# One layer of a conditioned trunk: second norm's root behind one modulation piece, transposes into bank pairs, ranking between queries, last rows loaded apart

## The chip, the cores and the metric

One Trainium2 chip, one of its cores. The metric is the device time of one execution of the program in microseconds (us), the median of several runs. The kernel before takes 3288.12 us, the median of three runs from 3284.90 to 3293.25. The profiled execution took 3291.78 us.

The engines are called as in the profile: PE multiplies matrices, PEld loads its weights, DVE works on vectors, ACT evaluates functions with a scale and a bias, POOL is the general engine that also issues the gathers, SP issues most DMAs.

## The reference

One layer, for 512 prompt rows (NA below) and 64 sample rows (8 groups of 8), with 2048 features each. It is cut here to what the change touches:

```python
mod = (silu(c) @ w_ada + b_ada).reshape(c.shape[0], 6, D_MODEL)
shift1, scale1, gate1, shift2, scale2, gate2 = [mod[:, k] for k in range(6)]
...
mix = concat([rmsnorm(out_lru), rmsnorm(out_sc)]) @ w_out
x = x + gate1 * mix
h2 = modulate(rmsnorm(x, norm2_g), shift2, scale2)
x = x + gate2 * peer(h2)
y = rmsnorm(x, final_g)
```

In `peer` each row has 8 heads. A head's query has two halves; each half is scored against 128 keys, the 16 best of each half make 256 candidates, and the 16 best of these pick 16 of 16384 experts. A pick multiplies the row with the expert's row of u, passes it through gelu and adds the expert's row of v, weighted.

## The kernel before, in words

All activations lie transposed: features on the 128 partitions, 16 chunks k of 128 features, the 576 rows along the free axis. Products that need full precision are made of three: every operand is split into a high and a low half (hhi, hlo; whi, wlo), and `mm3` (L131 to 139) multiplies high by high, low by high and high by low.

**Modulation pieces.** `w_ada` is read in 96 pieces of 1 MB (`ada_mm`, L181 to 192: load, four products into the bank `ada`, and after each fourth piece a copy `part` by ACT). `ada_out` (L194 to 208) transposes `part` into the bank `pm`, and DVE makes `pms` and the columns of `mods` of it. `ada_turn(n, keep)` (L351 to 361) does up to n pieces, leaves the last `keep` alone, and first finishes what is pending. The pieces are spread over the first stages as filling for PE.

**The w_out loop** (L611 to 630) runs over k: project chunk k into the PSUM tile `pp_o`, add the gated result to the row chunk `xk` to get `x1` (L622, L623 for the prompt rows, L624, L625 for the sample rows), write it to `x1d`, square it (L219) and add the squares into `sqa_n` (L220), and scale `x1` in place for the norm (L628, L629). An `ada_turn(1)` ends each pass.

**Norm 2.** `norm_stats` (L224 to 231) sums the squares over partitions on PE (`pc_n`, L228) and makes the reciprocal root `rc_n` on DVE and ACT (`rstd`, L140 to 149). `spread` (L233 to 241) multiplies it out over the partitions (`st_n`, L236, L238), and ACT copies it to `R_n` (L239, L240). Between the two stand `ada_turn(2, 0)` twice. Then the pieces that are left are done, and the last `pm` is transposed.

**The q loop** (L652 to 665), four passes q of four chunks each: `modulate` makes `m_h` (L283, DVE, every third chunk on POOL), `hhi` (L284, ACT) and `hlo` (L285, DVE); `mm3` adds these chunks into the first query's two banks `qa`; then PE transposes the new chunks back to rows, for the gathers' use, into `wide`, one tile of four banks, a bank for each 128 prompt rows i (L659). ACT copies the banks in pairs, after i = 1 and i = 3, to `h2s` (L663), and SP writes them to `h2d` (L665). `wide` has one buffer.

**The query stage** (L966 to 980) runs over seven heads: two projections each into a bank `qa` and a third of `wide`, ACT's copies, scores `sc`, and DVE's choice of the 16 best. From heads 0 to 3 DVE also counts how often a key scores high (`cnt`, L750). `rank_keys` (L930 to 959) is a generator in four parts: constants, the sum of the counts (`rk<-cnt`, L943), its transposition and the comparison (L948 on), and the permutation `perm` with `blk`, the order in which blocks of experts are read. The first part is run ahead of head 1, the other three after head 3, at high priority. Up to here PE's order in the w_out and q loops is as written; the other engines' order, and all of the query stage, is set by a scheduler.

**U and V stages** follow a schedule that is written out by hand: for each block of experts of the order `blk`, `pu` (L1367) and `pv` (L1387), with `xhi` and `xlo` (L900, L901) as halves of the loaded rows. Picks that miss the blocks are gathered row by row by POOL (L1197) and summed by DVE (u L1225, accB L1252), and the sums are scattered into `accd` in DRAM (L1267). `v_sum` (L1405 to 1421) adds a column `pv` of 128 features x 512 rows into `acc` (L1409), for eleven groups of heads (4, nine of 8, 4).

**The end.** In the last group (M - 4 to M - 1 of the M steps; `last` is M - 9) each column also takes in the gathered rows: `tok`, four tiles of 128 rows, loaded from `accd` at step last + 4 (L1725), transposed by PE onto `pv` (L1391). `v_sum` then scales by gate2 and adds (L1411), squares (L1415), writes the column to `x2d` (L1416), and sums the squares (L1421). `token_norm` (L1423 to 1438) makes the root of the last norm and spreads it into the bank `prfa`, copied to `sqs`, which is R (L1436). The last loop (L1758 to 1766) scales the 16 columns by `final_g` and R, every third one by ACT (L1762) and POOL (L1763), the others by DVE (L1765), and SP writes each to `y` (L1766).

Of the kernel before, what the change touches and what calls it, by code (L numbers as in the profile page):

```python
# [5 lines left out]
F32 = mybir.dt.float32  # L6
# [74 lines left out]
def build(ctx, tc, A, O, dbg=None):  # L81
# [532 lines left out]
    for k in range(KD):  # L614
# [9 lines left out]
        V.tensor_tensor(s3(x1[:, k, NP:]), s3(p[:, 1, NX:HT]), ctx_b(g1, k), op=ALU.mult)  # L624
        V.tensor_add(x1[:, k, NP:], x1[:, k, NP:], xk[:, NP:])  # L625
# [4 lines left out]
        ada_turn(1)  # L630
# [3 lines left out]
    ada_turn(2, 0)  # L634
    ada_turn(2, 0)
# [10 lines left out]
    wide = psum["p"].tile([128, 4, 512], F32, name="wide", tag="hT", bufs=1)  # L646

# [4 lines left out]
    for q in range(4):  # L652
# [3 lines left out]
        for i in range(NA // 128):  # L656
            for k in range(4):
                for p in range(2):
                    PE.matmul(wide[:, i, k * 128:(k + 1) * 128], hv[p][:, 4 * q + k, i * 128:(i + 1) * 128], idr,  # L659
                              start=p == 0, stop=p == 1)  # L660
            if i % 2:
                with tc.high_priority():
                    S.activation(t[:, i - 1:i + 1, :], wide[:, i - 1:i + 1, :], AF.Copy)  # L663
        for i in range(NA // 128):
            nc.sync.dma_start(h2d[i * 128:(i + 1) * 128, q * 512:(q + 1) * 512], t[:, i, :])  # L665
    pe1.close()
    dump("x1", x1)
# [250 lines left out]
    def query_banks(h, p):  # L918
        return [pbank("u", f"qa{h}{p}", 2)[:, :HT], wide[:, (2 * h + p) % 3, :HT]]
# [42 lines left out]
    for h in range(HD - 1):  # L962
        for p in range(2):
# [3 lines left out]
            if h or p:  # L967
                his, los = stream_w(A["wq"][2 * h + p], f"q{h}{p}")
                mm3(pq, his, los, movs)
            query_out(h, p, pq)  # L970
# [3 lines left out]
        if h == HEADS_COUNTED - 1:  # L974
            with tc.high_priority():
                run(ranking)
# [61 lines left out]
    def sample_rows():  # L1038

        hT = first_h["h"] = psum["p"].tile([128, D], F32, name="hT0", tag="hT", bufs=1)  # L1040
# [159 lines left out]
    def gather_u(i):  # L1200
# [8 lines left out]
        def use_h():  # L1209
            st["h"] = psum["p"].tile([128, D], F32, name=f"hT{i}", tag="hT", bufs=1)  # L1210
# [23 lines left out]
    def gather_v(i):  # L1234
# [7 lines left out]
        def add(j):  # L1242
            r, a = held.pop(j)
            row_log[a] = True
            if j == 0:
                S.activation(dots[i], dots[i], AF.Gelu_apprx_tanh)
                V.tensor_mul(dots[i], dots[i], gwt[i])
                st["a"] = psum["p"].tile([128, D], F32, name=f"accB{i}", tag="hT", bufs=1)
# [155 lines left out]
    def v_sum(gi, k, pv):  # L1404
# [5 lines left out]
        else:  # L1410
# [5 lines left out]
            nc.sync.dma_start(x2d[:, k, :], ak)  # L1416
            if k == 0:
# [5 lines left out]
    def token_norm(sq, n, nm, pool, banks):  # L1423
# [14 lines left out]
        return R  # L1438

    def finish_b():  # L1440
# [9 lines left out]
        ph = psum["p"].tile([128, D], F32, name="ph", tag="hT", bufs=1)  # L1450
# [257 lines left out]
    fplan = {(last + 1, 2), (last + 2, 3), (last + 3, 1), (last + 3, 3), (last + 4, 1), (last + 4, 3)}  # L1708
    NT = len(uses)
    cost = [FULL_ROWS if j < NU + bound[0] else 1.0 for j in range(NV0, NT)]  # L1710
    sums = [sum(cost[:j + 1]) for j in range(len(cost))]
    for m in range(M):
# [8 lines left out]
        if m == last + 4:  # L1721
            fin["tok"] = []
            for t in range(QT):
                r = new_row(f"tok{t}")[0]
                nc.sync.dma_start(r, accd[t * 128:(t + 1) * 128, :])  # L1725
# [175 lines left out]
```

## Time and profile before

| what | value |
|---|---|
| median of three runs | 3288.12 us (3284.90, 3288.12, 3293.25) |
| profiled execution, its own time | 3291.78 us |
| its span | 3290.0 us |
| mean granted PE clock | 0.972 |
| busy POOL / ACT | 1711.0 us (52%) / 1056.4 us (32%) |
| HBM read / written | 879.89 MB / 66.81 MB, 288 GB/s over the span |
| chain that ended last, shares | PE 42%, DMA 14%, issue 5%, DVE 4%, POOL 3%, ACT 1% |

A row of the waits reads: engine, tile and line that waited, the engine, tile and line that it waited for, the time in all, how many times, the longest. A row of the timeline reads: start, duration, engine, line, operation, tile written and tiles read, shapes, count, and in brackets the idle time before it and what ended that. A row of the windows gives for each engine its busy time and the count of instructions, then the granted PE clock, the busy share of the DMA engines and what they moved. In the tile names of the trace `x` is x1 as well as the chunks added to it, and `sqs` are the three tiles of the last norm.

### The profile page before, as it was taken

The numbers are of one execution on the slowest core, as the hardware profiler recorded it, in microseconds if no ns is written. First come the engines' busy times: TensorE is split into PE (matmuls) and PEld (weight loads), VectorE is DVE, ScalarE is ACT, GpSimd is POOL, SyncE is SP. The second block draws the span as 40 slices with busy tenths as digits, with TensorE's granted clock in tenths as the row PEclk, the third lists the DMA queues.
The fourth block names the chain that finished last, engine by engine and source line by source line (L and its number), as shares of the span: only waits on it lengthen the run. The fifth ranks groups of instructions, "written<-read, shape, count | busy, mean of one in ns | idle before, by whom it ended". The sixth has DMA issues, their size and how long they took to land.

```text
span 3290.0 us, 46694 instructions
## 1 busy us (share of the span) xinstructions
PE 3098.8 (94%) x17239; PEld 2625.0 (80%) x17239; DVE 2200.9 (67%) x3265; ACT 1056.4 (32%) x1645; POOL 1711.0 (52%) x1000
## 2 busy tenths in 40 slices
PE   6899999999979999999999998998999998989897
PEld 2688898999969998887788887886887777767676
DVE  3465521153345898896998989866777786877845
ACT  3244311132232232232565555642322222122122
POOL 2233233344333235667556665656677686676742
PEclk8999999999979999999999999999999999999998
DMA  9744565624432227989779898989999988998963
GB/s 378 259 144 134 165 220 199 223 93 132 130 129 80 71 85 251 309 311 380 311 307 388 357 374 318 395 289 388 394 367 395 389 326 308 346 351 322 373 201 142
DMA packets 297067, 882.84 MB, mean 268 GB/s; under 512 B 37590, under 2 KB 79446, under 8 KB 245366
## 3 DMA queue, kind: packets, MB, share of 16 engines
q1 hardware_dynamic: 161760, 382.48, 33.5%
q0 software_dynamic: 66336, 413.41, 31.8%
q10 hardware_dynamic: 68736, 83.90, 7.2%
q8 instruction: 136, 2.23, 0.3%
q14 instruction: 99, 0.81, 0.1%
HBM read 879.89 MB, written 66.81 MB: 288 GB/s over the span
## 4 chain that ended last, share of the span: by engine, by line
PE 42%; DMA 14%; issue 5%; DVE 4%; POOL 3%; ACT 1%; ACTq 0%; SPq 0%; POOLq 0%; DVEq 0%
PE pu L1367 17%; PE pv L1387 15%; DMA gsb<-gd 5%; DMA raw<-v 3%; PE qa L139 3%; DMA v<-v,rows 3%; PE wide L139 3%; PE gbank L1565 2%; POOL xlo L901 2%; DMA actr<-actd 2%; DMA u<-u,rows 1%; DVE u L1225 1%; POOL u L1197 1%; DVE accB L1252 1%; PE sc L736 0%
## 5 line engine op out<-in xcount | busy, mean ns | idle before, releaser
L901 POOL TENSOR_TENSOR xlo<-raw,xhi 128x1024 fp32r<-128x1024 f32 x320 | 777.1, 2441 | 455.8 <-ACT xhi L900 451.1
L900 ACT ACTIVATE xhi<-raw 128x1024 fp32r<-128x1024 f32 x320 | 338.5, 1060 | 873.4 <-PE pv L1387 418.3
L1252 DVE SCALAR_TENSOR_TENSOR accB<-v,dots,accB 128x2048 f32<-128x2048 f32 x211 | 496.4, 2353 | 160.5 <-DMA v<-v,rows 155.7
L1225 DVE SCALAR_TENSOR_TENSOR u<-u,hT 128x2048 f32<-128x2048 f32 x223 | 505.0, 2283 | 139.1 <-DMA u<-u,rows 137.1
L1387 PE MATMUL pv<-ahi,xhi 128*128 128x512 f32 x1280 | 515.3, 403 | 49.9 <-DVE acc L1409 38.5
L1387 PE MATMUL pv<-ahi,xlo 128*128 128x512 f32 x1280 | 510.7, 399 | 6.0 <-POOL xlo L901 6.0
L1367 PE MATMUL pu<-hhi,xhi 128*128 128x512 f32 x1280 | 515.8, 403 | 0.0
L1367 PE MATMUL pu<-hhi,xlo 128*128 128x512 f32 x1280 | 503.1, 393 | 5.9 <-POOL xlo L901 5.9
L1387 PE MATMUL pv<-alo,xhi 128*128 128x512 f32 x1280 | 507.7, 397 | 0.0
L1367 PE MATMUL pu<-hlo,xhi 128*128 128x512 f32 x1280 | 504.7, 394 | 0.0
L1387 PEld LDWEIGHTS pv<-ahi,xhi 128*128 128x128 f32 x1280 | 244.3, 191 | 115.5 <-DVE acc L1409 28.8
L1197 POOL DMA_INDIRECT u<-u,rows x223 | 226.0, 1014 | 201.9 <-DVE u L1225 154.3
L1197 POOL DMA_INDIRECT v<-v,rows x223 | 261.9, 1175 | 81.3 <-issue 37.5
L1387 PEld LDWEIGHTS pv<-ahi,xlo 128*128 128x128 f32 x1280 | 244.0, 191 | 66.1 <-POOL xlo L901 8.9
L1367 PEld LDWEIGHTS pu<-hhi,xlo 128*128 128x128 f32 x1280 | 241.7, 189 | 60.9 <-POOL xlo L901 6.8
L1387 PEld LDWEIGHTS pv<-alo,xhi 128*128 128x128 f32 x1280 | 244.8, 191 | 54.5
L1367 PEld LDWEIGHTS pu<-hhi,xhi 128*128 128x128 f32 x1280 | 242.5, 189 | 50.6 <-issue 0.9
L1367 PEld LDWEIGHTS pu<-hlo,xhi 128*128 128x128 f32 x1280 | 242.4, 189 | 47.4
L1559 ACT ACTIVATE op<-op,it 128x128 f32<-128x128 f32 x512 | 155.9, 389 | 72.4 <-DVE op L1551 70.0
L1565 PEld LDWEIGHTS gbank<-wr,op 128*128 128x128 f32 x1024 | 134.6, 193 | 39.5 <-ACT stg L1572 29.9
L1565 PE MATMUL gbank<-wr,op 128*128 128x80 f32 x1024 | 133.4, 274 | 23.5 <-ACT stg L1572 23.2
L128 POOL TENSOR_TENSOR wlo_q<-raw_q,whi_q 128x1024 fp32r<-128x1024 f32 x28 | 67.4, 2406 | 152.2 <-ACT whi_q L126 148.6
(481 smaller groups left out, 5512.0 us busy)
## 6 DMA issues: line engine op xcount, KB each, us to landing
wa<-w_ada SPq DMA_DIRECT2D x96, 1024.0 KB
raw<-ut SPq DMA_DIRECT2D x160, 512.0 KB
raw<-v SPq DMA_DIRECT2D x320, 256.0 KB
actd<-act ACTq DMA_DIRECT2D x80, 256.0 KB
gd<-stg ACTq DMA_DIRECT2D x64, 320.0 KB
gsb<-gd ACTq DMA_DIRECT2D x80, 256.0 KB
actr<-actd ACTq DMA_DIRECT2D x40, 512.0 KB
raw_o<-w_out SPq DMA_DIRECT2D x32, 512.0 KB
```

Source lines behind the costliest of these rows:

```text
L128: lo_engine(share).tensor_sub(lo, raw, r32(hi))
L139: PE.matmul(o, st, mv[pick](k), start=first, stop=last)
L900: S.activation(hi, raw, AF.Copy)
L901: G.tensor_sub(lo, raw, r32(hi))
L1197: G.indirect_dma_start(out=out, out_offset=None, in_=src, in_offset=bass.IndirectOffsetOnAxis(ap=idx, axis=0), bounds_check=NE * 128 - 1, ...
L1225: V.scalar_tensor_tensor(r, r, 1.0, st["h"], op0=ALU.mult, op1=ALU.mult, accum_out=dots[i][:, j:j + 1])
L1252: V.scalar_tensor_tensor(st["a"], r, dots[i][:, j:j + 1], st["a"], op0=ALU.mult, op1=ALU.add)
L1367: PE.matmul(pu, st[:, kk, :], movA[mv](k), start=k == 0 and a == 0, stop=k == KD - 1 and a == 2)
L1387: PE.matmul(pv, st, mv, start=first and j == 0 and a == 0, stop=last and not end and j == SG - 1 and a == 2)
L1559: S.activation(ops[:, j0 + j, :], ops[:, j0 + j, :], AF.Copy, scale=it[2][:, b * 4 + j:b * 4 + j + 1])
L1565: PE.matmul(pg[:, j * L:(j + 1) * L], ops[:, j0 + j, :], wr[:, j0 + j, :], start=True, stop=True)
```

## The change

It has five parts.

1. *Norm 2.* The sample rows' gated product is left in PSUM and added from there. `ada_turn(1, 6)` leaves six pieces instead of seven, so one more is done in the w_out loop; between root and spread stands one call of `ada_turn` for one piece, where two calls for up to two pieces each stood.
2. *Banks.* `wide` becomes a pool of its own with two-bank tiles in two buffers, one for each pair of i. It is closed after the loop, and the query stage gets a pool with four banks `qb` of its own. The tile `hT` and its successors move to a third pool.
3. *Ranking.* After query 0 of head 4, query 1 of head 4 and query 0 of head 5 one part of the generator is run, instead of the three parts after head 3.
4. *Gathered rows.* The four loads of `tok` stand at columns 0 and 2 of step last + 3 and of step last + 4.
5. *Last scaling.* ACT scales every third column (k % 3 == 1) right after its write to `x2d`, in place; `token_norm` also returns the bank that holds R, and DVE reads R there; POOL multiplies the scaled columns; odd columns are written to `y` by ACT's queue.

```diff
-        V.tensor_tensor(s3(x1[:, k, NP:]), s3(p[:, 1, NX:HT]), ctx_b(g1, k), op=ALU.mult)
-        V.tensor_add(x1[:, k, NP:], x1[:, k, NP:], xk[:, NP:])
+        V.tensor_tensor(s3(p[:, 1, NX:HT]), s3(p[:, 1, NX:HT]), ctx_b(g1, k), op=ALU.mult)
+        V.tensor_add(x1[:, k, NP:], p[:, 1, NX:HT], xk[:, NP:])
...
-        ada_turn(1)
+        ada_turn(1, 6)
     w_q = stream_w(A["wq"][0], "q00")
     ada_turn(2, 0)
     spread = norm_stats(st, D, "n2")
-    ada_turn(2, 0)
-    ada_turn(2, 0)
+    ada_turn(1, 0)
     R = spread()
...
-    wide = psum["p"].tile([128, 4, 512], F32, name="wide", tag="hT", bufs=1)
+    psw = ExitStack()
+    wp = psw.enter_context(tc.tile_pool(name="psw", bufs=1, space=PSUM))
...
         for i in range(NA // 128):
+            if i % 2 == 0:
+                wide = wp.tile([128, 2, 512], F32, name=f"wide{q}{i}", tag="wide", bufs=2)
             for k in range(4):
                 for p in range(2):
-                    PE.matmul(wide[:, i, k * 128:(k + 1) * 128], hv[p][:, 4 * q + k, i * 128:(i + 1) * 128], idr,
+                    PE.matmul(wide[:, i % 2, k * 128:(k + 1) * 128], hv[p][:, 4 * q + k, i * 128:(i + 1) * 128], idr,
                               start=p == 0, stop=p == 1)
             if i % 2:
                 with tc.high_priority():
-                    S.activation(t[:, i - 1:i + 1, :], wide[:, i - 1:i + 1, :], AF.Copy)
+                    S.activation(t[:, i - 1:i + 1, :], wide, AF.Copy)
...
     pe1.close()
+    psw.close()
+    psq = ExitStack()
+    qp = psq.enter_context(tc.tile_pool(name="psq", bufs=1, space=PSUM))
...
-        return [pbank("u", f"qa{h}{p}", 2)[:, :HT], wide[:, (2 * h + p) % 3, :HT]]
+        return [pbank("u", f"qa{h}{p}", 2)[:, :HT], qp.tile([128, 512], F32, name=f"qb{h}{p}", tag="qb", bufs=4)[:, :HT]]
...
                 mm3(pq, his, los, movs)
+            if 0 <= 2 * h + p - 2 * HEADS_COUNTED < 3:
+                with tc.high_priority():
+                    next(ranking)
             query_out(h, p, pq)
...
-        if h == HEADS_COUNTED - 1:
-            with tc.high_priority():
-                run(ranking)
...
             nc.sync.dma_start(x2d[:, k, :], ak)
+            if k % 3 == 1:
+                S.activation(ak, ak, AF.Copy, scale=cols[:, C_FG + k:C_FG + k + 1])
...
-        return R
+        return (R, pr[:, :n]) if nm == "a" else R
...
+    tplan = {(last + 3, 0), (last + 3, 2), (last + 4, 0), (last + 4, 2)}
...
-        if m == last + 4:
-            fin["tok"] = []
-            for t in range(QT):
-                r = new_row(f"tok{t}")[0]
-                nc.sync.dma_start(r, accd[t * 128:(t + 1) * 128, :])
-                fin["tok"].append(r)
...
+            if (m, kq) in tplan:
+                t = len(fin["tok"])
+                r = new_row(f"tok{t}")[0]
+                nc.sync.dma_start(r, accd[t * 128:(t + 1) * 128, :])
+                fin["tok"].append(r)
...
-        if k % 3 == 2:
-            S.activation(ak, ak, AF.Copy, scale=fg)
+        if k % 3 == 1:
             G.tensor_mul(ak, ak, R)
         else:
-            V.scalar_tensor_tensor(ak, ak, fg, R, op0=ALU.mult, op1=ALU.mult)
-        nc.sync.dma_start(O["y"][:, k, :NA], ak)
+            V.scalar_tensor_tensor(ak, ak, fg, Rp, op0=ALU.mult, op1=ALU.mult)
+        (nc.scalar if k % 2 else nc.sync).dma_start(O["y"][:, k, :NA], ak)
```

The order of PE between the w_out loop and the first query, before (`ada` is the bank that collects four pieces `wa` of a quarter vector, `part` its copy, `pm` its transposition; `pc_n`, `rc_n`, `st_n` belong to norm 2, `qa` to the first query):

```order
L228 MATMUL pc_n_8157<-ones,sqa_n_6369 128x1 x5
L189 MATMUL ada_2_5773<-wa_2_3_8171,cpad 32x512 x4
L199 MATMUL pm_2_8179<-ident,part_2_8177 128x128 x4
L189 MATMUL ada_3_8187<-wa_3_0_8188,cpad 32x512 x4
L189 MATMUL ada_3_8187<-wa_3_1_8194,cpad 32x512 x4
L236 MATMUL st_n_0_8201<-ident,rc_n_8163 128x128 x4
L238 MATMUL st_n_1_8202<-ident,rc_n_8163 128x64
L189 MATMUL ada_3_8187<-wa_3_2_8210,cpad 32x512 x4
L189 MATMUL ada_3_8187<-wa_3_3_8216,cpad 32x512 x4
L199 MATMUL pm_3_8224<-ident,part_3_8222 128x128 x4
L139 MATMUL qa_8241<-hhi,whi_q_0_8135 128x288
```

And now, on the same engine at the same place:

```order
L189 MATMUL ada_2_5773<-wa_2_3_8157,cpad 32x512 x4
L228 MATMUL pc_n_8165<-ones,sqa_n_6369 128x1 x5
L199 MATMUL pm_2_8179<-ident,part_2_8163 128x128 x4
L189 MATMUL ada_3_8187<-wa_3_0_8188,cpad 32x512 x4
L236 MATMUL st_n_0_8195<-ident,rc_n_8171 128x128 x4
L238 MATMUL st_n_1_8196<-ident,rc_n_8171 128x64
L189 MATMUL ada_3_8187<-wa_3_1_8204,cpad 32x512 x4
L189 MATMUL ada_3_8187<-wa_3_2_8210,cpad 32x512 x4
L189 MATMUL ada_3_8187<-wa_3_3_8216,cpad 32x512 x4
L199 MATMUL pm_3_8224<-ident,part_3_8222 128x128 x4
L139 MATMUL qa_8243<-hhi,whi_q_0_8141 128x288
```

The two products that make `st_n` stand behind one piece and one transposition, where they stood behind three pieces and one transposition; the piece `wa_2_3` is now ahead of `pc_n`, since every piece has moved up by one and one is done in the w_out loop.

ACT at the same place, before (`x` is the in-place scaling of the last chunk of x1, `R_n` the copy of the spread root, `ms_h_0` the sample rows of chunks 0 to 3):

```order
L192 ACTIVATE part_2_8177<-ada_2_5773 128x512
L628 ACTIVATE x_6307<-x_6307,mod_3369 128x512
L239 ACTIVATE R_n_8200<-st_n_0_8201 128x512
L240 ACTIVATE R_n_8200<-st_n_1_8202 128x64
L284 ACTIVATE hhi<-m_h_1_8248,mod_4442 128x512
L284 ACTIVATE hhi<-m_h_0_8244,mod_4442 128x512
L245 ACTIVATE hhi<-ms_h_0_8243 128x4x64
L284 ACTIVATE hhi<-m_h_2_8252,mod_4442 128x512
L284 ACTIVATE hhi<-m_h_3_8256,mod_4442 128x512
L192 ACTIVATE part_3_8222<-ada_3_8187 128x512
L284 ACTIVATE hhi<-m_h_4_8328,mod_4442 128x512
L284 ACTIVATE hhi<-m_h_5_8332,mod_4442 128x512
```

And now:

```order
L144 ACTIVATE rc_n_8171<-rc_n_8171 128x5
L239 ACTIVATE R_n_8194<-st_n_0_8195 128x512
L240 ACTIVATE R_n_8194<-st_n_1_8196 128x64
L628 ACTIVATE x_6307<-x_6307,mod_3369 128x512
L284 ACTIVATE hhi<-m_h_0_8246,mod_4442 128x512
L284 ACTIVATE hhi<-m_h_1_8250,mod_4442 128x512
L245 ACTIVATE hhi<-ms_h_0_8245 128x4x64
L284 ACTIVATE hhi<-m_h_2_8254,mod_4442 128x512
L284 ACTIVATE hhi<-m_h_3_8258,mod_4442 128x512
L284 ACTIVATE hhi<-m_h_4_8332,mod_4442 128x512
L284 ACTIVATE hhi<-m_h_5_8336,mod_4442 128x512
L192 ACTIVATE part_3_8222<-ada_3_8187 128x512
```

The last `part` copy, `part_3`, has moved behind the `hhi` of chunks 4 and 5; the scaling of `x` has moved behind the two copies of the root.

PE in the projection during which the sum of the counts is made, before (`rk` is the ranking's bank, `cnt` the counts, `qa` and `wide` the banks of the projection):

```order
L139 MATMUL qa_10080<-hlo,whi_q_0_10083 128x288
L139 MATMUL qa_10080<-hhi,wlo_q_0_10085 128x288
L943 MATMUL rk_9929<-cnt,ones 128x128
L139 MATMUL qa_10080<-hhi,whi_q_0_10083 128x288
L139 MATMUL wide<-hhi,whi_q_0_10083 128x288
L139 MATMUL wide<-hlo,whi_q_0_10083 128x288
```

And now, `qb` being the second bank:

```order
L139 MATMUL qb_10092<-hhi,whi_q_0_10095 128x288
L139 MATMUL qa_10091<-hlo,whi_q_0_10095 128x288
L947 MATMUL rk_10084<-cnt,ones 128x128
L139 MATMUL qb_10092<-hlo,whi_q_0_10095 128x288
L139 MATMUL qa_10091<-hhi,wlo_q_0_10097 128x288
L139 MATMUL qb_10092<-hhi,wlo_q_0_10097 128x288
```

The product of the counts is row 3943 of PE's order in both, the transposition `rk<-ident,rk_row` row 3952 in both; the last product, `rk<-rk_low,rowi`, has moved from row 3967 to row 4049. The banks of the projection alternate now where one was filled ahead of the other.

More of the change, by code (lines that the diff above doesn't have):

```diff
@@ L1038, in sample_rows @@
     def sample_rows():
-        hT = first_h["h"] = psum["p"].tile([128, D], F32, name="hT0", tag="hT", bufs=1)
+        psq.close()
+        psum["h"] = ctx.enter_context(tc.tile_pool(name="ps3", bufs=1, space=PSUM))
+        hT = first_h["h"] = psum["h"].tile([128, D], F32, name="hT0", tag="hT", bufs=1)
         for k in range(KD):
@@ L1209, in use_h @@
         def use_h():
-            st["h"] = psum["p"].tile([128, D], F32, name=f"hT{i}", tag="hT", bufs=1)
+            st["h"] = psum["h"].tile([128, D], F32, name=f"hT{i}", tag="hT", bufs=1)
             r, a = held.pop("h")
@@ L1247, in add @@
                 V.tensor_mul(dots[i], dots[i], gwt[i])
-                st["a"] = psum["p"].tile([128, D], F32, name=f"accB{i}", tag="hT", bufs=1)
+                st["a"] = psum["h"].tile([128, D], F32, name=f"accB{i}", tag="hT", bufs=1)
                 V.tensor_scalar(st["a"], r, dots[i][:, 0:1], None, op0=ALU.mult)
@@ L1449, in finish_b @@
         yield
-        ph = psum["p"].tile([128, D], F32, name="ph", tag="hT", bufs=1)
+        ph = psum["h"].tile([128, D], F32, name="ph", tag="hT", bufs=1)
         for k in range(KD):
@@ L1708, in build @@
     fplan = {(last + 1, 2), (last + 2, 3), (last + 3, 1), (last + 3, 3), (last + 4, 1), (last + 4, 3)}
+    fin["tok"] = []
+    tplan = {(last + 3, 0), (last + 3, 2), (last + 4, 0), (last + 4, 2)}
     NT = len(uses)
@@ L1755, in norm_banks @@
         return pbank("u", f"pcf{nm}", 2), pbank("g", f"prf{nm}", 2)
-    R = drive(token_norm(fin["sq"], NA, "a", vp, norm_banks("a")))
+    R, Rp = drive(token_norm(fin["sq"], NA, "a", vp, norm_banks("a")))
     for k in range(KD):
```

## The prediction

> **What bounds the kernel now.** I read the page first, then the windows of the whole program, then the waits of the stages that the change touches, then their timelines. On the page, the span and the busy shares:
>
> ```profile
> span 3290.0 us, 46694 instructions
> PE 3098.8 (94%) x17239; PEld 2625.0 (80%) x17239; DVE 2200.9 (67%) x3265; ACT 1056.4 (32%) x1645; POOL 1711.0 (52%) x1000
> ```
>
> The profiled execution took 3291.78 us, 1.8 more than its span and 3.7 more than the median of 3288.12; the sum below is made against 3291.78. PE is busy for 94% of it, so a gain must come from the 191 us in which PE stands, or from stretches in which it runs at a lower clock. The same, by stages (start:end, length, busy time of PE, PEld, DVE, ACT, POOL, granted clock, DMA share, GB/s):
>
> ```profile
> 943.00:1000.00 57.00, 47.30 (x262) 46.37 (x263) 18.83 (x28) 20.03 (x28) 22.93 (x16) 0.72 0.28 95
> 1000.00:1110.00 110.00, 109.98 (x822) 106.92 (x821) 72.31 (x465) 27.85 (x50) 35.80 (x15) 1.00 0.22 73
> 1110.00:1217.00 107.00, 100.96 (x729) 98.46 (x728) 104.44 (x448) 23.06 (x43) 34.03 (x14) 0.97 0.23 75
> 2290.00:3180.00 890.00, 844.22 (x3596) 676.78 (x3595) 684.64 (x395) 199.56 (x187) 609.36 (x361) 0.99 0.92 345
> ```
>
> The first is the q loop behind norm 2: 10 us idle and a mean clock of 0.72, the worst of the four. The second is the query stage, full to the brim. Who is waited for in the q loop, and how its windows of 3.4 us follow each other:
>
> ```profile
> PE wide L659 <- ACT h2s L663: 8.6, 5, 4.0
> 950.40:953.80 3.40, 0.00 (x0) 0.00 (x0) 3.37 (x5) 2.64 (x4) 2.69 (x3) 1.00 0.00 0
> 953.80:957.20 3.40, 3.33 (x16) 3.33 (x16) 3.16 (x3) 1.35 (x3) 3.24 (x4) 0.52 0.40 154
> 957.20:960.60 3.40, 3.40 (x16) 3.40 (x16) 1.34 (x2) 0.50 (x2) 2.76 (x3) 0.50 0.00 0
> 960.60:964.10 3.50, 2.93 (x24) 2.70 (x23) 2.63 (x5) 2.94 (x5) 0.09 (x1) 0.98 0.14 54
> 964.10:967.50 3.40, 1.64 (x15) 1.50 (x15) 1.40 (x2) 2.42 (x3) 3.40 (x3) 1.00 0.29 111
> 967.50:970.90 3.40, 3.40 (x17) 3.40 (x17) 0.00 (x0) 1.02 (x1) 3.40 (x3) 0.51 0.39 146
> 970.90:974.30 3.40, 3.40 (x16) 3.40 (x16) 0.00 (x0) 0.00 (x0) 2.49 (x2) 0.50 0.00 0
> 974.30:977.70 3.40, 2.34 (x20) 2.20 (x19) 0.00 (x0) 1.02 (x1) 0.00 (x0) 0.98 0.86 249
> 977.70:981.10 3.40, 3.35 (x16) 3.35 (x17) 0.00 (x0) 0.00 (x1) 0.00 (x0) 0.52 0.56 214
> 981.10:984.50 3.40, 3.40 (x16) 3.40 (x16) 0.00 (x0) 1.02 (x1) 0.00 (x0) 0.50 0.36 141
> ```
>
> Three windows hold over a microsecond of idle PE time (3.40, 1.76 and 1.06 us). Behind each stand two at clock 0.5, each doing in 3.4 us what takes 1.7 at full clock. A wait there costs itself and about 3.4 us more: six slow windows, 10.2 us.
>
> **The change part by part.** *The norm's root (ctx part through PSUM, one ada piece earlier).* The timeline round it:
>
> ```profile
> 920.75 2.31 DVE L625 TENSOR_TENSOR x<-x,xk 128x64 f32<-128x64 f32 x1
> 928.75 3.64 PE L189 MATMUL ada<-wa,cpad 128*32 128x512 f32 x16
> 932.33 1.68 PE L236 MATMUL st_n<-ident,rc_n 128*128 128x128 f32 x8
> 934.05 0.60 ACT L239 ACTIVATE R_n<-st_n 128x512 f32<-128x512 f32 x1 [5.78 <-PE st_n L236]
> 940.57 0.58 ACT L192 ACTIVATE part<-ada 128x512 f32<-128x512 f32 x1
> 943.66 1.33 ACT L284 ACTIVATE hhi<-m_h,mod 128x512 fp32r<-128x512 f32 x2 [2.52 <-POOL m_h L283]
> 941.20 1.12 PE L199 MATMUL pm<-ident,part 128*128 128x128 f32 x4 [3.53 <-ACT part L192]
> ```
>
> L625 takes 2.31 us for 64 columns with both operands in SBUF; with one from PSUM at most that can go, and the sum of squares behind it, whose operands stay in SBUF, may take the delay over: 0 to 2 us, I take 1. Then st_n stands behind one ada piece instead of three. The two that move away are worth one row: 3.64 us for two pieces, 1.82 each at the clock that they had. So R comes some 4.6 us earlier, near 929.4. None of it need reach PE: the last pm waits for the last ada part, and in the new order ACT does that part behind two more hhi, which in before begin at 943.66, 9.6 us behind R. With R at 929.4 these two end near 940.3, the part ends near 940.9, and pm begins near 941, as now. The piece that moves into the PE-bound k loop costs 0.9 us (half of 1.82, at full clock); one piece less stands behind the loop, where PE waits 3.53 us anyway. I take 0 for the part, between 1 lost (the piece, with nothing back) and 5 won (all of R's lead). If the hhi come later than that, PE's projections start later with them, which is the lost end.
>
> *Banks in pairs.* PE's third block of transposes no longer waits for the copy of the first two blocks, only for the copy of its own pair, a loop pass earlier. That removes the 8.6 us and the 10.2 behind them, 18.8. The copies themselves are still late once: ACT's order has them behind two hhi of 0.67, and the next query's banks open only when the last copy is out, as now:
>
> ```profile
> 992.17 0.61 PE L139 MATMUL wide<-hhi,whi_q 128*128 128x288 f32 x1 [1.11 <-ACT h2s L663]
> ```
>
> That wait stays, and I let one more of its size with its slow stretch (1.1 + 3.4) stay inside the loop: 14.3 us. Bounds: 18.8 if none is left, 5.3 if three are. The Trainium skill's page "TensorE: Matmul & The Clock Gate" (HAM oscillation, and its table of advice) says that only gaps of about 3 us and more bring the clock down. The trace disagrees: idle times of 1.76 and 1.06 us have the same two slow windows behind them as that of 3.40. If the rule held, short waits would not be what slows those windows, and this part would give 7.5; that is the first rival.
>
> *Query banks of their own* (four instead of three quarters of the wide tile) change nothing in a stage where PE is busy 109.98 of 110 us.
>
> *Ranking behind three queries.*
>
> ```profile
> 1115.21 0.77 PE L943 MATMUL rk<-cnt,ones 128*128 128x128 f32 x2 [4.85 <-DVE cnt L750]
> ```
>
> PE stands 4.85 us for DVE's count. In the new order the product of the count stands in the same row of PE's 13,000, the transposition too; only the third product moves 82 rows back, and no wait is shown there. DVE, 104.4 of 107 us busy, reaches its count no earlier against PE. I take 0; 8 if the wait and a slow stretch (4.85 + 3.4) went after all, and 1 lost if DVE's copies come late for the block numbers.
>
> *Gathered rows apart.*
>
> ```profile
> 3184.00:3188.00 4.00, 4.00 (x19) 3.03 (x18) 1.46 (x2) 0.22 (x1) 3.18 (x2) 1.00 0.56 197
> 3188.55 2.36 SPq L1725 DMA_DIRECT2D tok<-accd  x4
> PE pv L1391 <- DMA tok<-accd: 5.4, 3, 2.0
> 3197.06 0.38 PE L1391 MATMUL pv<-ident,tok 128*128 128x128 f32 x2
> 3204.91 5.12 PE pv L1387 x12
> 3211.04 2.79 PE pv L1387 x12
> ```
>
> Four loads of 1 MB begin at 3188.55; the first is used at 3197.06, the others are waited for. Two now start a step earlier, where the DMA queues are half idle (0.56), and two where all four were, with half the bytes ahead: the last two should land about when the first two did, at 3197 to 3199. The waits cost 5.4 us and the slow clock behind them 2.3 (5.12 for the same twelve products that take 2.79 a column later): 7.7. It is half of that if the last tile is still late, and a little more, 8.5, if the pairs between the waits also run at full clock. SP issues nothing later than before: xf goes from behind four of these loads to behind two and two.
>
> *The last scaling.*
>
> ```profile
> 3271.00 12.46 DVE L1765 SCALAR_TENSOR_TENSOR acc<-acc,cols,sqs 128x512 f32<-128x512 f32 x11 [2.86 <-ACT sqs L1436]
> 3227.03 0.74 DVE L1411 SCALAR_TENSOR_TENSOR acc<-pv,mod,acc 128x512 f32<-128x512 f32 x1
> 3270.00:3274.00 4.00, 0.33 (x2) 0.04 (x1) 3.00 (x3) 3.63 (x6) 2.35 (x2) 0.50 0.20 74
> 3282.00:3286.00 4.00, 0.00 (x0) 0.00 (x0) 1.46 (x3) 0.00 (x0) 0.00 (x0) 0.50 1.03 381
> 3286.00:3290.00 4.00, 0.00 (x0) 0.00 (x0) 0.00 (x0) 0.00 (x0) 0.00 (x0) 0.50 0.31 118
> 912.78 0.72 ACT L628 ACTIVATE x<-x,mod 128x512 f32<-128x512 f32 x1 [1.76 <-DMA x1d<-x]
> ```
>
> Eleven columns take 12.46 us, 1.13 each, from SBUF alone beside POOL. With R in PSUM a column has the operands of L1411, 0.74: 8.1 us, and they begin 0.6 earlier, since DVE no longer waits for ACT's copy of R (0.60, as the copy of R_n above, of the same shape). That would be 5.0. But the output is 4.2 MB, 11.0 us at the 381 GB/s of the only full window. Before, its traffic begins near 3273.2 (0.20 of that window, at its end) and ends near 3287.3 (0.31 of the last). It would now begin at 3272.6 and end at 3283.6: 3.7 us won. Bounds 3 and 5. Half of the writes move to ACT's queue, which has nothing else to do there. The scaling that ACT does early waits for the column's own write; it stood 1.76 us for such a write in the k loop and then took 0.72, together less than the 2.79 us that PE needs for a column's first twelve products. It is hidden; if the write took twice as long it would cost about 1.5 us in each of five columns.
>
> *Between them.* 14 us won at 990 must pass through 2200 us of query, U and V stages. All their loads are released by PE, DVE or POOL work of the same stage, so I let them shift whole.
>
> The sum: 0 + 14.3 + 0 + 7.7 + 3.7 = 25.7, so 3266.1 for the profiled execution and 3262.4 against the median; I say 3262.
>
> **The rivals.** *The clock stays low in the q loop.* Not the short waits but the kind of work (transposes with little in them) would hold the clock down; then two of the three slow pairs of windows, 6.8 us, stay. For it: the slow windows are filled with transposes (x16). Against: the slow rows behind 1.06 us of idle, and the projections of the window before it, which run at 0.98. 25.7 less 6.8 is 18.9: 3269. Chance 0.15.
>
> *The lead is lost on the way.* In U and V the DMA share is 0.92, and who sets the pace there may be bytes rather than PE. Then only the end counts, 7.7 + 3.7 = 11.4: 3277. Against it PE's 844 busy of 890. Chance 0.13.
>
> *The ranking works.* If DVE is ahead by as much as the norm's lead, the 4.85 and the slow stretch go as well, 8.2: 33.9 in all, 3254. Chance 0.07.
>
> *Slower: the V stage falls out of step.* Rows of the stage:
>
> ```profile
> DVE accB L1252 <- DMA v<-v,rows: 133.4, 52, 9.9
> PE pv L1387 <- DVE acc L1409: 38.5, 20, 5.5
> ```
>
> DVE does PE's sums and the gathered rows' sums in one queue. When a gathered row is late, up to 9.9 us, PE's sum stands behind it and PE's banks fill; that already costs 38.5 us. A shift of 14 us moves gathers against weight loads; were each of the nine groups of eight to get one more wait of the longest kind, 9 x 5.5 = 50 us would come on, and the total would be 3288 - 26 + 50 = 3312. It decides from 26 us of new waits on, five such. Against it: gathers and sums are placed by PE's steps and not by time. Chance 0.05.
>
> **How the numbers follow.** The forecast itself has 0.60. A measurement of this kernel tells 0.3% from no change, 9.9 us: faster is below 3278.2, slower above 3298. The forecast's own bounds (5.3 to 18.8, 3.9 to 8.5, 3 to 5, and -1 to 5 for the norm, not all at one end) run from 3252 to 3275. The lost lead at 3277, give or take 4, must be taken in, and the ranking at 3254: 3250 to 3280 leaves out the slower case and the edges, under 0.2. Faster: 0.57 + 0.14 + 0.08 + 0.07 = 0.86; same: 0.03 + 0.01 + 0.05 = 0.09; slower: 0.05.
>
> **What would show it.** In the new profile: PE's waits for h2s at 0 to 2 us instead of 8.6, and one slow pair of windows or none between 950 and 990; R_n near 929 to 930 but the first projection still near 942; the wait for cnt unchanged at 4.8; waits for the gathered rows under 1 us; the eleven last columns in about 8 us and the output ending about 11 us after its first byte. The prediction is wrong if PE's waits in the V stage move by more than 10 us either way, if the q loop keeps a clock near 0.7 without waits, or if ACT waits for the x2d writes beyond a column's pitch.

## The result, and the profile after

The changed kernel takes 3276.97 us, the median of twelve runs (3261.30 to 3283.48), beside 3294.31 for the kernel before, of twelve as well (3284.90 to 3303.69). The ratio is 0.994, 95% interval 0.9925 to 0.9954: 15 to 25 us won, 20 most likely (the two medians are 17.3 apart). The forecast was 25.7 and a time of 3262, in a range of 3250 to 3280. Of the 15 us between 3262 and 3277, 6 are the base: the three runs of before that the sum was set against had a median of 3288.12, and twelve have 3294.31.

The profiled execution took 3275.15 us. Its page:

```profile
span 3273.3 us, 46692 instructions
PE 3088.6 (94%) x17239; PEld 2616.8 (80%) x17239; DVE 2173.3 (66%) x3265; ACT 1056.9 (32%) x1645; POOL 1718.4 (52%) x1000
```

The span is 16.7 us shorter, PE's busy time 10.2: part of the gain is idle time, part is work that now runs at full clock.

**Norm 2.** The timeline between the w_out loop and the first query, of the changed kernel:

```profile
920.99 0.22 DVE L625 TENSOR_TENSOR x<-pp_o,xk 128x64 f32<-128x64 f32 x1
921.96 1.74 DVE L220 TENSOR_TENSOR sqa_n<-sqa_n,sq_n 128x576 f32<-128x576 f32 x1 [0.75 <-ACT sq_n L219]
927.79 1.93 PE L236 MATMUL st_n<-ident,rc_n 128*128 128x128 f32 x8
929.75 0.60 ACT L239 ACTIVATE R_n<-st_n 128x512 f32<-128x512 f32 x1 [4.28 <-PE st_n L236]
939.37 1.33 ACT L284 ACTIVATE hhi<-m_h,mod 128x512 fp32r<-128x512 f32 x2 [2.98 <-POOL m_h L283]
940.61 0.57 ACT L192 ACTIVATE part<-ada 128x512 f32<-128x512 f32 x1
941.23 1.12 PE L199 MATMUL pm<-ident,part 128*128 128x128 f32 x4 [6.98 <-ACT part L192]
```

L625 fell from 2.31 us to 0.22, and the sum of squares behind it took over a part of that (1.74 where it took 0.76). It seems to be POOL that holds them: before, its subtraction for `wlo_q` ran from 920.62 to 922.97, and L625, with both operands in SBUF, ended at 923.06; now it runs from 920.74 to 923.10, L625 with one operand in PSUM passes beside it in 0.22 us, and the sum of squares, still in SBUF alone, ends at 923.70. R comes at 929.75 instead of 934.05. PE sees nothing of it at this place: the last `pm` begins at 941.23, where it began at 941.20, and its wait has doubled, 6.98 us for 3.53.

**The q loop.** PE's waits in it, and its windows:

```profile
PE wide L660 <- ACT h2s L664: 1.8, 1, 1.8
PE qb L139 <- ACT h2s L664: 1.1, 1, 1.1
PE qa L139 <- ACT qt L927: 3.0, 1, 3.0
953.80:957.20 3.40, 2.16 (x20) 2.02 (x18) 3.03 (x4) 1.93 (x4) 1.28 (x1) 1.00 0.40 154
957.20:960.60 3.40, 2.81 (x22) 2.81 (x23) 3.03 (x5) 2.89 (x5) 1.68 (x1) 0.93 0.40 154
960.60:964.00 3.40, 3.40 (x18) 3.40 (x17) 0.00 (x0) 1.75 (x2) 3.40 (x3) 0.56 0.42 159
964.00:967.40 3.40, 3.40 (x33) 3.40 (x32) 0.00 (x0) 1.03 (x1) 3.40 (x3) 1.00 0.00 0
...
981.00:984.40 3.40, 1.51 (x10) 1.51 (x11) 0.65 (x5) 0.71 (x2) 0.00 (x0) 0.95 0.23 78
984.40:987.80 3.40, 3.40 (x17) 3.40 (x16) 0.00 (x0) 0.31 (x1) 0.00 (x0) 0.55 0.00 0
```

One wait for a copy is left of five, and one slow window stands behind it instead of six. (The two further executions of the kernel before have four slow windows there: the pair behind the wait of 1.06 us was that one execution's own.) The transposes of 964 to 967.40 do 33 products in the time that 16 took: it was the waiting, not the kind of work, that held the clock down. The third row is new in size: PE waits until ACT has emptied the first query's banks, and another slow window follows. Who held ACT:

```profile
982.43 0.41 ACT L927 ACTIVATE qt<-qa 128x288 f32<-128x288 f32 x1 [6.54 <-DMA h2d<-h2s]
982.89 0.40 PE L139 MATMUL qa<-hhi,whi_q 128*128 128x288 f32 x1 [2.97 <-ACT qt L927]
```

ACT's first copy of a query waits for the last writes to `h2d`: their source `h2s` lies in a pool that is closed there, and the query's tile is put in its place. ACT stood for this before too, 4.77 us, but PE was then still busy with slow products.

**The ranking.** PE still stands in front of the sum of the counts:

```profile
1100.81 0.76 PE L947 MATMUL rk<-cnt,ones 128*128 128x128 f32 x2 [4.83 <-DVE cnt L754]
```

**The end.** The gathered rows of the first column, with the loads of the last two tiles and the queues while they were under way, and the last scaling:

```profile
3182.25 0.84 SPq L1742 DMA_DIRECT2D tok<-accd  x2
3184.00:3188.00 4.00, 4.00 (x19) 3.29 (x18) 2.09 (x4) 1.06 (x1) 0.14 (x1) 1.00 1.05 404
3190.84 0.83 PE L1397 MATMUL pv<-ident,tok 128*128 128x128 f32 x6
3193.44 0.49 PE L1397 MATMUL pv<-ident,tok 128*128 128x128 f32 x2 [1.77 <-DMA tok<-accd]
3227.24 0.72 ACT L1424 ACTIVATE acc<-acc,cols 128x512 f32<-128x512 f32 x1 [3.30 <-DMA x2d<-acc]
3240.27 0.72 ACT L1424 ACTIVATE acc<-acc,cols 128x512 f32<-128x512 f32 x1 [1.38 <-DMA x2d<-acc]
3247.87 0.72 ACT L1424 ACTIVATE acc<-acc,cols 128x512 f32<-128x512 f32 x1 [1.39 <-DMA x2d<-acc]
3257.42 7.33 DVE L1773 SCALAR_TENSOR_TENSOR acc<-acc,cols,prfa 128x512 f32<-128x512 f32 x11 [2.86 <-ACT sqs L1444]
3262.00:3266.00 4.00, 0.00 (x0) 0.00 (x0) 2.75 (x5) 0.00 (x0) 1.63 (x2) 0.50 1.03 379
3266.00:3270.00 4.00, 0.00 (x0) 0.00 (x0) 0.00 (x0) 0.00 (x0) 0.00 (x0) 0.50 1.03 383
```

Three tiles are there in time, the fourth is 1.77 us late: it was issued 9 us ahead of its use into full queues. The eleven columns take 7.33 us for 12.46 and are done at 3264.75; the output at 380 GB/s sets the end, and from 3266 on no engine computes. DVE still waits 2.86 us in front of the columns, for ACT's copy, although it reads the bank and not the copy: the forecast's 0.6 for that did not come. The early scalings were meant to be hidden; here the chain that ended last runs through the last two of them and the writes that they wait for, 2.00 us each.

**Where the lead went in between.** The first product of the U stage and the first product with gathered rows, before and after (median and extreme durations in ns, then the first and last start):

```profile
L1367 PE MATMUL pu<-hhi,xhi x1280: 387/393/774, 1216.6 to 2268.7; 128*128 128x512 f32 x183
L1391 PE MATMUL pv<-ident,tok x128: 270/275/582, 3197.1 to 3262.2; 128*128 128x128 f32 x128
```

```profile
L1373 PE MATMUL pu<-hhi,xhi x1280: 387/393/774, 1200.5 to 2261.8; 128*128 128x512 f32 x183
L1397 PE MATMUL pv<-ident,tok x128: 270/275/377, 3190.8 to 3248.8; 128*128 128x128 f32 x128
```

The lead, the time by which the changed kernel is ahead, is 16.1 us where the U stage begins and 6.4 where the gathered rows come in. Between these points the kernel before took 1980.5 us, the changed one 1990.3. Nothing in the waits of the U and V stages stands out. Either these stages take a lead back, or their length scatters; this was the main question for the experiments.

### The profile page after: what moved, and what is told of

Read it like the earlier page. It is cut to its first block, busy times and chain, and to the rows that moved or that the text cites. A ratio compares the mean times of both kernels' runs of the same rounds, so it can differ in the third digit from the quotient of the medians.

```text
span 3273.3 us, 46692 instructions
## 1 busy us (share of the span) xinstructions
PE 3088.6 (94%) x17239; PEld 2616.8 (80%) x17239; DVE 2173.3 (66%) x3265; ACT 1056.9 (32%) x1645; POOL 1718.4 (52%) x1000
## 4 chain that ended last, share of the span: by engine, by line
PE 67%; DMA 15%; DVE 7%; issue 4%; POOL 4%; ACT 2%; ACTq 0%; SPq 0%; POOLq 0%; DVEq 0%
PE pu L1373 19%; PE pv L1393 14%; PE pp_o L139 6%; DMA v<-v,rows 4%; DMA gsb<-gd 4%; PE pp_c L139 3%; PE pp_s L139 3%; PE qa L139 3%; PE pp_b L139 3%; PE qb L139 3%; PE gbank L1573 2%; PE pp_x L139 2%; PE pp_y L139 2%; PE ada L189 2%; POOL xlo L905 2%
## 5 line engine op out<-in xcount | busy, mean ns | idle before, releaser
L905 POOL TENSOR_TENSOR xlo<-raw,xhi 128x1024 fp32r<-128x1024 f32 x320 | 785.6, 2467 | 453.8 <-ACT xhi L904 440.5
L1393 PE MATMUL pv<-ahi,xhi 128*128 128x512 f32 x1280 | 514.8, 402 | 43.7 <-DVE acc L1415 33.7
L1393 PE MATMUL pv<-ahi,xlo 128*128 128x512 f32 x1280 | 510.8, 399 | 10.7 <-POOL xlo L905 10.5
L1203 POOL DMA_INDIRECT v<-v,rows x223 | 260.4, 1168 | 77.9 <-issue 36.3
L1373 PEld LDWEIGHTS pu<-hlo,xhi 128*128 128x128 f32 x1280 | 243.0, 190 | 47.8
L1573 PE MATMUL gbank<-wr,op 128*128 128x80 f32 x1024 | 133.6, 274 | 25.7 <-ACT stg L1580 25.5
```

The costliest lines, as they stand in the source:

```text
L905: G.tensor_sub(lo, raw, r32(hi))
L1203: G.indirect_dma_start(out=out, out_offset=None, in_=src, in_offset=bass.IndirectOffsetOnAxis(ap=idx, axis=0), bounds_check=NE * 128 - 1, ...
L1373: PE.matmul(pu, st[:, kk, :], movA[mv](k), start=k == 0 and a == 0, stop=k == KD - 1 and a == 2)
L1393: PE.matmul(pv, st, mv, start=first and j == 0 and a == 0, stop=last and not end and j == SG - 1 and a == 2)
L1573: PE.matmul(pg[:, j * L:(j + 1) * L], ops[:, j0 + j, :], wr[:, j0 + j, :], start=True, stop=True)
```

## The experiments

Four places are read in each profiled execution: the start of the U stage, the time from there to the first gathered-row product ("middle"), from there to the 13th column's ("rows"), and from there to the end of the span ("tail").

| kernel | U start | middle | rows | tail |
|---|---|---|---|---|
| before, three executions | 1216.6, 1214.1, 1215.5 | 1980.5, 1987.0, 1989.8 | 53.3, 53.8, 51.6 | 39.6, 38.8, 38.8 |
| changed, three executions | 1200.5, 1202.4, 1201.5 | 1990.3, 1988.6, 1991.2 | 46.1, 46.2, 48.2 | 36.3, 35.6, 35.6 |
| norm and banks alone | 1200.4 | 1982.7 | 50.3 | 38.8 |
| banks alone | 1204.2 | 1996.0 | 53.0 | 38.8 |
| end alone | 1211.5 | 1992.0 | 49.1 | 35.5 |
| changed, ranking as before | 1201.3 | 1993.5 | 46.9 | 35.7 |
| two more pieces in the loop | 1202.2 | 1991.8 | 49.9 | 36.4 |
| banks for the second query | 1194.6 | 1983.8 | 48.4 | 35.4 |
| gathered rows a step earlier | 1202.2 | 1986.7 | 46.9 | 38.8 |
| these three together | 1197.7 | 1983.7 | 47.8 | 38.0 |

**Norm and banks alone.** The kernel before with the first two parts of the diff and nothing else:

```diff
+        ada_turn(1, 6)
...
+                wide = wp.tile([128, 2, 512], F32, name=f"wide{q}{i}", tag="wide", bufs=2)
```

> The kernel before with the norm-2 part and the bank part alone (ranking, gathered rows and last scaling as before). My theory: the first product of the U stage comes about 15 us earlier (1201 to 1203 instead of 1216.6), nearly all from the waits for the copies, and the end keeps its waits (5 us for gathered rows, 12.5 us for the last columns). If the U and V stages only scatter from one execution to the next, the total is 0.4 to 0.5% below before. Rival: the U and V stages give back 6 to 10 us of any lead; then the total is 0.2% below or less.

Ratio to before 0.9954 (0.9937 to 0.9970): 15 us. The U stage starts at 1200.4, and the middle took 1982.7 us with a full lead of 14. My theory held, the rival did not: 0.2% lies outside the interval.

**The end alone.** The kernel before with the gathered rows apart and the last scaling:

```diff
+    tplan = {(last + 3, 0), (last + 3, 2), (last + 4, 0), (last + 4, 2)}
...
+            V.scalar_tensor_tensor(ak, ak, fg, Rp, op0=ALU.mult, op1=ALU.mult)
```

> The kernel before with the gathered rows apart and the last scaling alone. My theory: nothing ahead of the last group moves (first product of the U stage at 1216 to 1217), the last group is 7 us shorter and the last scaling 3.3 us: 0.3% below before. Rival: the earlier loads of the gathered rows take the queues from the v loads, and the steps ahead of the last group lose what the group wins; then there is no difference.

Ratio 0.9975 (0.9959 to 0.9991): 8 us, rather than 10. The tail is 3.3 to 4.1 us shorter, as expected, the rows stretch 2.5 to 4.7, where I had expected 7. The rival, no difference, lies outside the interval. Its middle, without any of the edits ahead, took 1992.0, so a long middle doesn't need a lead. That its U stage starts at 1211.5, with a program that is the same up to there, shows how much this place moves by itself: 5 us.

**Banks alone.** As the first, without the norm's part:

```diff
         V.tensor_add(x1[:, k, NP:], x1[:, k, NP:], xk[:, NP:])
...
         ada_turn(1)
```

> The kernel before with the bank part alone. My theory: the norm part is worth nothing at PE, so the first projection of the q loop starts near 942.8 as before, and the lead at the U stage is that of the kernel with both parts within 2 us. Rival: R's lead of 4 to 5 us is what lets the copies come in time; then the pairs alone leave two to three waits for the copies with their slow windows, and the lead is 8 us or less.

Ratio 0.9974 (0.9963 to 0.9985), 9 us; against 15 with both parts the intervals overlap slightly. The lead is 3.8 us smaller than with both. PE's waits, of this kernel:

```profile
PE wide L661 <- ACT h2s L665: 5.0, 1, 5.0
PE pm L199 <- ACT part L192: 4.0, 1, 4.0
PE qb L139 <- ACT h2s L665: 1.1, 1, 1.1
PE qa L139 <- ACT qt L928: 1.0, 1, 1.0
```

One wait for a copy of 5.0 us stands where the kernel with both parts has two of 2.6 together. So the truth lies between theory and rival: R's lead doesn't bring the first projection forward (944.4 here, 941.5 to 945.3 in the four executions without either part), but it brings the copies forward: the second of the loop starts at 962.45 on ACT here and at 958.10 with both parts. I had given the norm's part nothing and all of this to the banks. The wait is the firm part of this, 5.0 us against 1.6 to 2.6 in all seven executions with both parts and six pieces left; the 3.8 us at the U stage are one execution against another, at a place that moves by 5 by itself.

**The ranking as before.** The changed kernel with the third part undone:

```diff
-            if 0 <= 2 * h + p - 2 * HEADS_COUNTED < 3:
-                with tc.high_priority():
-                    next(ranking)
+        if h == HEADS_COUNTED - 1:
+            with tc.high_priority():
+                run(ranking)
```

> The changed kernel with the ranking as before (all of it after head 3). My theory: the same time as the changed kernel within 0.15%, and PE's wait for the counts 4.8 us as in both. Rival: the later order of the blocks disturbs the start of the U stage and costs the lead that is lost between U and V; then it is 0.2% faster than the changed kernel.

Ratio to before 0.9934 (0.9915 to 0.9954), beside 0.994 for the changed kernel; the U stage starts at 1201.3. The ranking's part is worth nothing that shows.

**Two more pieces in the w_out loop.** To see what holds the first projection:

```diff
-        ada_turn(1, 6)
+        ada_turn(1, 4)
```

> The changed kernel with two more modulation pieces in the w_out loop (four left instead of six), so that the last part's copy stands on ACT ahead of the second pair of hhi instead of behind the third. My theory: the last pm, which waits 7 us for that copy, is what holds the first projection at 942; it now starts near 937 to 939 (two pieces of 0.96 us later than it could), PE's 7 us wait is under 2, and the U stage starts 2 to 5 us earlier than in the changed kernel (1196 to 1199). Rival: the halves hhi and hlo bind the q loop; then PE starts earlier and waits inside the loop instead, and the second query starts no earlier than 975.

The profile of this kernel at the place in question:

```profile
937.43 1.11 PE L199 MATMUL pm<-ident,part 128*128 128x128 f32 x4 [2.87 <-ACT part L192]
938.19 0.59 PE L139 MATMUL qa<-hhi,whi_q 128*128 128x288 f32 x1
938.96 0.61 PE L139 MATMUL qa<-hhi,whi_q 128*128 128x288 f32 x1 [0.18 <-ACT hhi L245]
939.84 0.61 PE L139 MATMUL qa<-hlo,whi_q 128*128 128x288 f32 x1 [0.28 <-DVE hlo L285]
941.44 0.61 PE L139 MATMUL qa<-hlo,whi_q 128*128 128x288 f32 x1 [0.99 <-DVE hlo L246]
```

The copy of the last part did hold the first projection: it now starts at 938.19 instead of 942, though PE's wait for the copy is still 2.87 us. And the rival holds for the rest: PE then waits for the halves, the second query starts at 978.7 (975.9 to 980.0 in the changed kernel), the U stage at 1202.2. The halves are only 1.5 us of what is lost again: the waits for the copies are 3.4 us instead of 1.6 to 2.4, and the clock stays at half until 947.4, as it does until 946.6 to 949.7 in the changed kernel, so that what starts earlier runs slowly. Ratio 0.9940 (0.9919 to 0.9962): nothing won.

**Banks for the second query.** The wait for ACT's copy, taken away by other banks:

```diff
     def query_banks(h, p):
+        if (h, p) == (0, 1):
+            return [qp.tile([128, 512], F32, name=f"q{x}01", tag="qb", bufs=4)[:, :HT] for x in "ab"]
```

> The changed kernel with the second query in two of the four new banks, so that PE need not wait until ACT has emptied the first query's banks (ACT waits there for the last h2d writes, whose buffer becomes the query's). My theory: this wait took 1 to 4 us and a slow window after it in each kernel with paired banks; without it the U stage starts 3 to 5 us earlier, 1196 to 1198. Rival: PE only meets the same wait at the next query, and nothing is won.

ACT's wait at this place and PE's waits between 935 and 1015 us, of this kernel, without that for the last part:

```profile
ACT qt L929 <- DMA h2d<-h2s: 8.2, 1, 8.2
...
PE wide L660 <- ACT h2s L664: 1.8, 1, 1.8
...
PE qa L139 <- ACT h2s L664: 1.1, 1, 1.1
```

ACT still stands, for 8.2 us, but PE no longer does. The U stage starts at 1194.6, 7 us ahead of the mean of the changed kernel. Not all of that is the banks': in this execution no slow window stands in the loop at all, not even behind the wait of 1.8 us that stayed, where the three executions of the changed kernel have two or three in it. The kernel with all three edits, below, has the same banks, two slow windows behind its first wait, and a U stage that starts 3.8 us ahead. Ratio 0.9929 (0.9913 to 0.9945), median 3270.08: the fastest median of all, though its interval overlaps that of the changed kernel.

**Gathered rows a step earlier.**

```diff
-    tplan = {(last + 3, 0), (last + 3, 2), (last + 4, 0), (last + 4, 2)}
+    tplan = {(last + 3, kq) for kq in range(4)}
```

> The changed kernel with all four loads of gathered rows at the four columns of step last + 3. My theory: the 1.8 to 2.9 us that PE still waits for the last of these tiles go, and from the first gathered-row product to that of the ninth column it takes 15 us instead of 16.8 to 19.7; 3 us in all. Rival: the v loads queued behind them come late instead, and PE waits for xhi or xlo by as much.

No wait for a gathered row is left, and others have come. Of this kernel, the waits of the end:

```profile
DVE acc L1408 <- DMA xf<-x1d: 14.8, 2, 10.2
...
PE pcfa L1437 <- DVE sqs L1429: 4.8, 1, 4.8
```

DVE waits 14.8 us for `xf`, whose load stands behind these four on SP (7.2 to 10.4 us in the changed kernel's three executions), its sums are late at the last column, and PE waits 4.8 us for them where it waited 2.4 to 3.1. What DVE has lost it can't make up: the chain that ended last runs through three writes of x2d and the early scalings behind them. The rows take 46.9 us, as in the changed kernel (46.1 to 48.2); the tail is back at 38.8. Ratio 0.9938 (0.9917 to 0.9959). The rival named the wrong victim, the v loads, but held: the wait moved.

**All three.** The last three edits in one kernel:

```diff
+        ada_turn(1, 4)
...
+        if (h, p) == (0, 1):
...
+    tplan = {(last + 3, kq) for kq in range(4)}
```

> The changed kernel with these three edits together. My theory: they add up, 8 to 12 us under the changed kernel, 0.9 to 1.0% under the kernel before. Rival: the U and V stages take such leads back, and it is within 0.15% of the changed kernel.

Ratio 0.9927 (0.9913 to 0.9940), median 3271.19: no better than the second query's banks alone. The edits don't add up, and two of them showed no gain by themselves. The rival named 0.15%; it is 0.13% by the two ratios, whose intervals overlap.

**The same kernels again.** No edit; two more profiled executions each of before and after.

> The kernel before, unchanged, profiled once more. My theory: the 1980.5 us that its profiled execution took from the first product of the U stage to the first gathered-row product was at the short end of a scatter from 1980 to 1996 us; it now takes another value in there, near 1988, and the U stage starts at 1211 to 1217. Rival: without a lead the stage always takes 1980 to 1982, and the lead is what costs 8 us.

> As the first of these runs: the kernel before, unchanged, a third profiled execution.

Middles of 1987.0 and 1989.8 us, and a U start at 1214.1 and 1215.5: the theory held, the rival fell. The 1980.5 that the forecast was set against is the shortest of fourteen.

> The changed kernel, unchanged, profiled once more. My theory: the U stage starts at 1200 to 1202, and from there to the first gathered-row product it takes any value between 1980 and 1996 us. Rival: 1990 again, within 1.5.

> As the second of these runs: the changed kernel, unchanged, a third profiled execution.

Middles of 1988.6 and 1991.2 beside 1990.3: this kernel scattered little in three executions, nearly as the rival had it (1988.6 is 1.7 away). Over all fourteen, the four without a lead (before and the end alone) have a mean of 1987.3, the ten with one 1988.8, and single ones lie between 1980.5 and 1996.0. So 1.5 us of a lead of 13 may be lost there, with some 6 to either side that these few can't tell; by the three executions each of before and after alone it would be 4.3, which isn't told from 0 either. More than half of the 9.8 us of the first pair was chance. The times of all runs say the same in another way: 15 us for the front alone and 8 for the end alone make 23, beside 20 for both, each with 5 or so to either side.

## Why the prediction was right, and where it was off

Direction and range held. By stages, the means of the executions with a part against those without it (the three edits to the changed kernel are left out, since they touch these places; banks alone are left out of the first row):

| term | forecast | measured |
|---|---|---|
| norm and banks, up to the U stage | 14.3 | 13.2 (1214.4 to 1201.2) |
| ranking | 0 | 0 within the interval |
| gathered rows | 7.7 | 5.1 (52.4 to 47.3) |
| last scaling | 3.7 | 3.2 (39.0 to 35.7) |
| U and V stages | passed whole | 1.5 lost, not told from 0 |

That is 21.5 less 1.5, 20.0, and the ratio of 0.994 says 20. That the two agree so closely is luck, since the last row alone is uncertain by 6.

*The bound, and how waits were priced:* right as a mean, not wait by wait. A wait for a copy of 1.6 to 1.8 us had one or two slow windows behind it in four executions with paired banks and none in three (the ranking as before, the banks for the second query, the gathered rows a step earlier); one of 1.1 us had one in three of all ten executions with paired banks. Where the wait lies in the clock's windows decides (last section). The six slow windows that were priced were that execution's; the kernel before had four there in its others. The rival that the clock would stay low without waits fell with the row of 33 transposes at 1.00.

*The norm's part at nothing:* right at the place that was argued, R at 929.75 for 929.4 and pm at 941.23 for 941; wrong as a price. The step that failed is "None of it need reach PE": the lead reaches PE through the copies inside the loop, where the wait is 5.0 us without it and 1.6 to 2.6 with it; at the U stage the two executions differ by 3.8. The sum came out well because the banks' term had been worked out as if this were its own, and that is luck.

*The banks:* "I let one more of its size with its slow stretch stay inside the loop". It did, 1.8 us and one slow window. What wasn't seen is the wait for the first query's banks, 1.0 to 3.0 us, hidden before by slow products, and a slow window behind it or, where it was 1.0, behind the wait of 1.1 just ahead of it. The kernel that takes it away was 7 us earlier at the U stage in its one profiled execution, 4 in the kernel with all three edits.

*The ranking:* right, at the row that was named; the wait of 4.83 us is there, and undoing the part changes nothing.

*The gathered rows:* the mis-sized term. The step that failed is "the last two should land about when the first two did": the last two are issued 8 to 9 us ahead of their use, into queues whose share was 0.56 at that stretch and is 1.05 in the changed kernel, and PE gets the fourth 10.7 us after its issue. PE still waits, 1.8 to 2.9 us in the executions with this part as in the change, where under 1 was named. That the fuller queues are what delays them is argued, not shown; with all four loads ahead, no such wait was left. Nor did "SP issues nothing later than before" keep `xf` in time: its first load stands behind two tiles, and DVE waits 7.2 to 10.4 us for it, 1.8 to 2.4 in the executions without this part.

*The last scaling:* right, with its bound: the output's 11 us at 380 GB/s. The early scalings do wait, up to 3.30 us, and with their 0.72 that is 4.0, more than the 3.8 that a column takes (46.1 over twelve). "It is hidden" held in two executions of three, where PE waits 2.4 us for the last sum as in the kernel before; in the first it waits 3.1, behind the late `xf` and two of these scalings.

*The lead passing the U and V stages:* right as far as can be told. The rival in which bytes set the pace there had looked right on the first pair of profiles alone. The V stage's waits for DVE, 33.7 us where 38.5 were, did not grow.

## What to carry to other kernels

Before a term is worked out from one profile, have the same kernel's stages from two or three executions; here a stage of 1980 us scatters by 15, more than any single term of the sum. When a wait in front of an engine is taken away, look at once for what is late next: here the first wait behind it was a buffer reused across a pool's closing, invisible while the engine was slow, and two spare banks brought the U stage another 4 to 7 us forward, beside 13, in the two executions that had them. An operand's arrival that doesn't show at the first instruction behind it can still show ten steps on, in a copy that must pass the same queue.

## What the runs showed of the hardware

The granted clock drops after short idle times, and how short differs between two stages with different work. The clock changes in steps of 3.41 us; laid out in these windows, with the idle times in a window added up, over the fourteen profiled executions: in the U and V stages (1200 to 3190 us, products of 128 x 512), all 174 windows with over 2.0 us of idle PE time were followed by one at half clock, 31 of 106 with 1.5 to 2.0, and none of 300 with 0.5 to 1.5. In the q loop (transposes of 128 x 128 and products of 128 x 288), it was 28 of 30 with over 1.0 us and none of 34 with 0.5 to 1.0. Two cases of the kernel before, each window with the one behind it:

```profile
2793.70:2797.11 3.41, 1.51 (x7) 1.30 (x8) 3.41 (x3) 0.32 (x1) 3.08 (x3) 1.00 0.86 325
2797.11:2800.52 3.41, 3.41 (x16) 2.65 (x15) 3.41 (x3) 0.00 (x0) 3.41 (x2) 1.00 0.69 252
3196.49:3199.90 3.41, 1.44 (x8) 0.92 (x6) 0.56 (x1) 0.00 (x0) 2.76 (x2) 1.00 1.01 428
3199.90:3203.31 3.41, 0.80 (x2) 0.50 (x2) 0.00 (x0) 0.00 (x0) 0.00 (x0) 0.50 1.05 325
```

1.90 us idle left the clock alone, 1.97 brought it down. Where a wait lies in the windows decides as well. In the q loop with paired banks, three waits of 1.8 us for a copy left the clock alone, and a border between two windows had cut each into parts of 0.83 to 0.99 us; four of 1.6 to 1.8 us brought it down, and in each of these one window held 1.05 us or more. Of the waits of 1.11 us, the five that a border cut did nothing, and three of the five that lay in one window brought the clock down. No run places a wait on purpose. The Trainium skill's page "TensorE: Matmul & The Clock Gate" (its table of advice) advises to keep gaps under about 3 us; these runs put the limit at 1 to 2 us of idle time in a window, so the prediction's doubt of that rule stands.
